# A hybrid transformer block on one core: weight sums loaded a unit ahead, the merge begun with the second half of the tokens, the last part of top-k in more steps

## The chip, the core and the metric

The kernel runs on one core of a Trainium2 chip. The core has five engines that run their own instruction streams: TensorE (PE in the profile; its weight loads are PEld), VectorE (DVE), ScalarE (ACT), GpSimd (POOL), and SyncE (SP), which here only issues DMAs. The order of the instructions on each engine is fixed when the program is built; at run time an instruction waits for what it needs and holds back all that stand behind it on its engine. The metric is the device time of one execution in microseconds (us), lower being better.

## The reference

One layer on a sequence of 1024 tokens and a width of 1024, all in float32:

```python
x = x + 1/2 * SwiGLU_1(RMSNorm(x))            # FFN1, hidden width 2816
h = RMSNorm(x); P = h @ W_in                  # one projection for all that follows
A = DSA sparse attention                      # indexer scores -> top 256 keys -> 8 heads
M = mLSTM matrix memory                       # conv, chunks of 64, stabilised scan
x = x + W_out( sigmoid(g_a) * (A @ W_a) + sigmoid(g_b) * (M @ W_b) )
x = x + 1/2 * SwiGLU_2(RMSNorm(x))            # FFN2
...
top_s, top_i = lax.top_k(score, k_sel)        # 256 keys of each query, from the indexer's scores
```

`g_a` and `g_b` are two slices of `P`. The fifth line is called the merge below.

## The kernel before

**Matmuls.** Each float32 product is made of three matmuls of rounded parts (high by high, high by low, low by high: `mm3`, L769, L770, L771). Before that an operand is split into a high and a low part: ScalarE rounds it (L898, L452, L185, L297), VectorE or POOL subtracts (L899, L453, L186, L298). The large products are done with sums of quarter blocks (products 0 to 6 in place of 8), so that the weights have to be added up as well as the activations.

**FFN1 and the weight sums.** `gate_up` (about 60 to 440 us) multiplies by the gate and up weights, `Down` (440 to 600 us) by the down weights. Beside them, `Presums` makes the sums of two later weights: 19 units of columns of `w_in` during `gate_up` (`step`, called once per column pair) and 4 units of rows of `w_out` during `Down` (`step_rows`). A unit takes two buffers of 1024 columns from the segments `plain` and `more` (11 pages in all, which everything else in these stages uses too), two loads of 512 KB on SP's queue (L371 for columns), four VectorE sums of 128x512 (L376, L377, L379, L380 for columns, L352, L353, L355, L357 for rows) and four stores of 256 KB to `d_s` or `d_o` on the same queue. The generator yields between these parts, so that the load of a unit is placed a call ahead of its sums.

In `Down`, L634 adds a psum into a tile of `h`, L606 and L613 add and subtract such tiles on VectorE, and L648 does so on POOL, on 128x1024.

**Mixing.** The projections run beside the top-k search on VectorE and ScalarE. The generator `topk` yields a share of a step, by which the loop that runs it decides how much to place beside each piece of the projections. Its last part takes, for each block j of 128 queries, a mask of the 256 best keys: a count (L1540 to L1542), a scan (L1544), two combining operations (L1546, L1547), and two ScalarE copies. L1205, L1237 and L1242 are VectorE's evictions of the projections' psum there.

**Attention and merge.** The attention ends, at about 1362 us, in steps of two product matmuls (L2124, L2125), an eviction of 64x512 on ScalarE (L2079), a normalising VectorE operation (L2084) and the split into `swap` (L898, L899) for the next product. `proj_b` multiplies M by W_b beside it; its last operations are L1928 on VectorE, and it holds the segment `h0` through `ybT` until it ends. `merge` then goes over eight weight blocks n, each in two halves of 512 tokens (`th`):

```python
sa, tb = ar.alloc(1024), ar.alloc(1024)      # L2176, L2177: 512 KB each, both halves
with self.tc.issue_after(self.split_A):      # not ahead of the last split of the attention
    nc.scalar.activation(y[th][c].f, sa.f[:, cs], AF.Sigmoid)      # L2181; y lies in h0
self.proj(w, yaT, th, ps)                    # 12 matmuls of 128x512
v.tensor_tensor(a, a, ps, ALU.mult)          # L2187; L2188 adds tb
```

The weights of W_a come through L846 and L185, the prepared weight sums of `w_out` through L431 and L452. After the merge FFN2 runs like FFN1, without weight sums.

**What sets the order.** The calls are written in the order above, but a scheduler with a simulated timeline decides, when the program is built, how each engine's instructions interleave; `issue_after` forbids it to place an instruction ahead of a named one.

Of the kernel before, what the change touches and what calls it, by code (L numbers as in the profile page):

```python
# [22 lines left out]
AF = mybir.ActivationFunctionType  # L23
# [295 lines left out]
class Presums:  # L319
# [6 lines left out]
    def __init__(self, k, w_in, d_s, w_out, d_o):  # L326
        self.k, self.w_in, self.d_s, self.w_out, self.d_o = k, w_in, d_s, w_out, d_o
        self.order = list(dict.fromkeys(i[0] for i in MIXING if i != "ik"))
        self.work, self.more = self.steps(), self.rows()

    def two(self):
        two = [None, None]
        while not all(two):
            two = [self.k.ar.alloc(1024, soft=True) for _ in range(2)]
            if not all(two):
                for b in two:
                    if b:
                        b.free()
                yield
        return two  # L340

    def rows(self):
        k, nc = self.k, self.k.nc
        for j in range(4):
            two = yield from self.two()
            for h in range(2):
                with k.tc.issue_after(k.mark):
                    nc.sync.dma_start(two[h].f, self.w_out[h * 512 + j * P:h * 512 + j * P + P, :])
            yield
            b11, b12, b21, b22 = (b.f[:, c:c + 512] for b in two for c in (0, 512))  # L350
            op = nc.vector.tensor_tensor
            op(b11, b12, b11, ALU.subtract)  # L352
            op(b12, b22, b12, ALU.subtract)  # L353
            yield
            op(b22, b22, b11, ALU.subtract)  # L355

            op(b21, b21, b22, ALU.subtract)  # L357
            for q, b in ((4, b11), (6, b12), (5, b22), (3, b21)):
                nc.sync.dma_start(self.d_o[j, Outs.SLOT[q]], b)
            for b in two:  # L360
                b.free()

    def steps(self):
        k, nc = self.k, self.k.nc
        for p in self.order:
            two = yield from self.two()
            v = [b.f.rearrange("p (k y c) -> p k y c", k=4, y=2) for b in two]
            for h in range(2):
                src = self.w_in[h * 512:h * 512 + 512, PAIRS[p]:PAIRS[p] + 256].rearrange("(k p) c -> p k c", p=P)
                with k.tc.issue_after(k.mark):  # L370
                    nc.sync.dma_start(two[h].f.rearrange("p (k c) -> p k c", k=4), src)  # L371
            yield
            a11, a21 = (v[0][:, :, y] for y in range(2))
            a12, a22 = (v[1][:, :, y] for y in range(2))
            op = nc.vector.tensor_tensor
            op(a22, a21, a22, ALU.add)  # L376
            op(a21, a11, a21, ALU.subtract)  # L377
            yield
            op(a11, a22, a11, ALU.subtract)  # L379
            op(a12, a12, a11, ALU.subtract)  # L380
            for q, b in ((5, a11), (6, a21), (2, a12), (4, a22)):
                nc.sync.dma_start(self.d_s[p, self.SLOT[q]].rearrange("p (k c) -> p k c", k=4), b)
            for b in two:
                b.free()
# [298 lines left out]
class Block:  # L683
# [814 lines left out]
    def topk(self, js, share):  # L1498
# [29 lines left out]
        for j in range(n):  # L1528
# [22 lines left out]
            yield 0.4  # L1551
# [849 lines left out]
```

## Time and profile before

| | |
|---|---|
| three runs | 2120.27, 2124.79 and 2126.83 us, median 2124.79 us |
| profiled execution | own time 2123.45 us, span 2121.7 us from the first to the last instruction |
| busy | TensorE 96%, VectorE 78%, ScalarE 50%, POOL 18% of the span |
| mean granted TensorE clock | 0.990 |

The shares of busy time are means over stages with different limits. In a stage where TensorE is busy throughout, nothing else sets the time. Where its row has gaps, the view of its waits says which instruction of another engine it waited for, and that engine's own row says what that one had waited for. The granted clock of a stretch is the TensorE clock as a share of full speed.

### The profile page before, as it was taken

To read this page: it belongs to the slowest core of one execution; us is meant where nothing else is said; L and a number is where in the kernel's file an instruction comes from. 1 tells how busy PE (TensorE), PEld (TensorE's weight loads), DVE (VectorE), ACT (ScalarE), POOL (GpSimd) and SP (SyncE) were. 2 spreads that over 40 slices of the span, in tenths; PEclk is the share of its full clock that TensorE was granted. 3 is DMA by queue.
4 is the path that set the end of the run, shared out by engine and by line. 5 is a ranking of instruction groups with operands and counts; after the bars stand their busy time and mean duration, and the time that the engine had idled before them with its cause. 6 is when DMAs were issued, how large, how long until landed. Compare 5 with 4: busy or idle time off the path is not lost. (4 is left out here: it accounts for less than half of the span.)

```text
span 2121.7 us, 27881 instructions
## 1 busy us (share of the span) xinstructions
PE 2046.8 (96%) x9349; PEld 1675.9 (79%) x9349; DVE 1650.1 (78%) x2852; ACT 1055.6 (50%) x1968; POOL 383.5 (18%) x397
## 2 busy tenths in 40 slices
PE   7999999999999989999999999899999999999999
PEld 5788787888787768777777788688888888888887
DVE  7977887678866785998889788787987666669963
ACT  8332222334436564985786578745723333334442
POOL 1000000000304323343445545422000000000300
PEclk9999999999999999999999999999999999999999
DMA  5479885394644223366686312552333232377241
GB/s 184 145 248 300 274 273 163 130 359 137 213 136 140 75 76 102 107 182 176 179 270 201 110 50 76 208 194 77 122 134 110 94 110 100 109 276 265 90 144 40
DMA packets 281804, 338.30 MB, mean 159 GB/s; under 512 B 20941, under 2 KB 186429, under 8 KB 281661
## 3 DMA queue, kind: packets, MB, share of 16 engines
q1 hardware_dynamic: 281660, 336.53, 48.6%
q8 instruction: 73, 1.20, 0.2%
q14 instruction: 71, 0.57, 0.1%
HBM read 231.57 MB, written 104.89 MB: 159 GB/s over the span
## 5 line engine op out<-in xcount | busy, mean ns | idle before, releaser
L769 PE MATMUL psum<-h,round 128*128 128x512 f32 x656 | 261.5, 399 | 3.1 <-DVE plain L1061 2.2
L770 PE MATMUL psum<-h,round 128*128 128x512 f32 x656 | 259.8, 396 | 1.0 <-DVE h L899 0.8
L771 PE MATMUL psum<-h,round 128*128 128x512 f32 x656 | 258.6, 395 | 0.3 <-DVE round L298 0.3
L648 POOL TENSOR_TENSOR swap<-swap,h 128x1024 f32<-128x1024 f32 x12 | 32.8, 2771 | 1020.5 <-DVE h L634 1020.5
L512 POOL TENSOR_TENSOR round<-raw,round 128x512 fp32r<-128x512 f32 x108 | 147.7, 1374 | 155.9 <-ACT round L511 111.2
L769 PEld LDWEIGHTS psum<-h,round 128*128 128x128 f32 x656 | 124.3, 190 | 30.6 <-DVE plain L1061 2.8
L771 PEld LDWEIGHTS psum<-h,round 128*128 128x128 f32 x656 | 124.2, 189 | 27.8 <-issue 1.6
L770 PEld LDWEIGHTS psum<-h,round 128*128 128x128 f32 x656 | 124.4, 190 | 27.0 <-DVE h L899 1.5
L769 PE MATMUL psum<-swap,round 128*128 128x512 f32 x312 | 125.8, 404 | 11.2 <-DVE plain L1237 6.9
L770 PE MATMUL psum<-swap,round 128*128 128x512 f32 x312 | 124.1, 398 | 1.1 <-DVE swap L899 0.9
L771 PE MATMUL psum<-swap,round 128*128 128x512 f32 x312 | 123.8, 397 | 0.2 <-POOL round L512 0.2
L1563 DVE TENSOR_SCALAR_CACHE_REDUCE plain<-plain 128x384 bf16<-128x384 f32 (+1 forms) x124 | 100.3, 808 | 2.5
L898 ACT ACTIVATE round<-plain 128x512 fp32r<-128x512 f32 x74 | 46.2, 631 | 106.0 <-PE psum L770 98.7
L297 ACT ACTIVATE round<-plain 128x512 fp32r<-128x512 f32 x75 | 47.3, 632 | 94.4 <-PE psum L770 70.0
L511 ACT ACTIVATE round<-raw 128x512 fp32r<-128x512 f32 x108 | 66.6, 622 | 38.1 <-PE psum L770 26.0
L899 DVE TENSOR_TENSOR round<-plain,round 128x512 fp32r<-128x512 f32 x74 | 57.0, 776 | 32.6 <-ACT round L898 32.3
L769 PE MATMUL psum<-h,spare 128*128 128x512 f32 x200 | 78.8, 396 | 3.1 <-DVE plain L1061 2.6
L769 PEld LDWEIGHTS psum<-swap,round 128*128 128x128 f32 x312 | 59.8, 192 | 26.9 <-DVE plain L1237 7.8
L770 PE MATMUL psum<-h,spare 128*128 128x512 f32 x200 | 78.7, 393 | 1.9 <-DVE h L899 1.9
L769 PE MATMUL psum<-h,extra 128*128 128x512 f32 x200 | 78.3, 392 | 2.2 <-DVE plain L1205 1.6
L769 PE MATMUL psum<-side 128*128 128x512 f32 x204 | 79.4, 389 | 0.0
L770 PE MATMUL psum<-side 128*128 128x512 f32 x204 | 79.4, 389 | 0.0
(750 smaller groups left out, 6027.7 us busy)
## 6 DMA issues: line engine op xcount, KB each, us to landing
plain<-d_a SPq DMA_DIRECT2D x154, 256.0 KB
d_a<-plain SPq DMA_DIRECT2D x117, 256.0 KB
raw<-in_ffn_w_gate_dram SPq DMA_DIRECT2D x44, 512.0 KB
plain<-in_w_in_dram SPq DMA_DIRECT2D x37, 512.0 KB
d_s<-plain SPq DMA_DIRECT2D x74, 256.0 KB
raw<-d_s SPq DMA_DIRECT2D x74, 256.0 KB
h<-in_ffn_w_down_dram SPq DMA_DIRECT2D x66, 256.0 KB
raw<-in_w_in_dram SPq DMA_DIRECT2D x53, 256.0 KB
```

What stands on the lines that cost most here:

```text
L297: k.nc.scalar.activation(hi.r.rearrange("p (k c) -> p k c", k=4), src, AF.Copy)
L511: self.done_A = k.nc.scalar.activation(hi.r, raw.f, AF.Copy).ins
L512: k.nc.gpsimd.tensor_tensor(lo.r, raw.f, hi.f, ALU.subtract)
L648: k.nc.gpsimd.tensor_tensor(x(th, dh), x(th, dh), u, ALU.add)
L769: mm(ps, lhs[0], rhs[0], start=start, stop=False, skip_group_check=more)
L770: mm(ps, lhs[0], rhs[1], start=False, stop=False, skip_group_check=more)
L771: mm(ps, lhs[1], rhs[0], start=False, stop=stop, skip_group_check=more)
L898: self.split_A = self.nc.scalar.activation(hi, src, AF.Copy).ins
L899: self.nc.vector.tensor_tensor(lo, src, hi.bitcast(F32), ALU.subtract)
L1563: v.tensor_scalar(s.junk[:, :s.width[j]], s.sc[j], s.cand[:, j:j + 1], None, ALU.is_ge, ALU.add, accum_out=s.cnt[:, j:j + 1])
```

## The change

Three edits are made together. All arithmetic, all volumes and all other stages stay.

1. `Presums` holds one unit of work back: the generator `run` issues the loads of a unit, and only then the sums of the unit before. Two units, four pages, can be held at a time. If there is no room for the next unit's buffers, the waiting unit's sums go first. (The sums of columns are now L368, L369, L371 and L372, their loads L362; the sums of rows L392, L393, L395 and L397.)
2. `merge` takes the halves in another order: the second half of the tokens for n = 0 to 4, then the first half for n = 0 to 4, then both halves of n = 5 to 7. The pre-activations are loaded by half (256 KB instead of 512 KB), straight into their place in `h0`, and the sigmoid works in place. The sigmoids may now stand ahead of the last splits, but not ahead of the last exponential of the attention (`exp_A` instead of `split_A`). The weights of five blocks are held at a time.
3. The last part of `topk` is cut into five steps per block instead of three, with the same sum of shares (0.2 + 0.3 + 0.3 + 0.3 + 0.1 for 3 x 0.4). The two ScalarE copies become steps of their own, and two buffers are freed before the last of them.

```diff
+    def run(self, units):
+        waiting = []
+        for load, work in units:
+            while True:
+                two = [self.k.ar.alloc(1024, soft=True) for _ in range(2)]
+                if all(two):
+                    break
+                for b in two:
                     if b:
                         b.free()
+                if waiting:
+                    yield from waiting.pop(0)
                 yield
+            load(two)
+            yield
+            waiting.append(work(two))
+            if len(waiting) > 1:
+                yield from waiting.pop(0)
+        for w in waiting:
+            yield from w
...
             act.activation(sc[j], sc[j], AF.Copy, scale=one(s.sg, j))
+            yield 0.2
...
-            yield 0.4
+            yield 0.3
             v.tensor_tensor_scan(pre.f, eq.f, eq.f, 0.0, ALU.add, ALU.max)
-            yield 0.4
+            yield 0.3
             v.scalar_tensor_tensor(eq.f, pre.f, one(s.ngt, j), eq.f, ALU.is_le, ALU.mult)
             v.scalar_tensor_tensor(sc[j], sc[j], thr, eq.f, ALU.is_gt, ALU.add)
-            act.activation(sc[j], sc[j], AF.Copy, bias=NEG, scale=-NEG)
             eq.free()
             pre.free()
-            yield 0.4
+            yield 0.3
+            act.activation(sc[j], sc[j], AF.Copy, bias=NEG, scale=-NEG)
+            yield 0.1
...
-                nc.scalar.activation(p.f, p.f, AF.Exp, bias=nb, scale=sc, accum_out=su)
+                self.exp_A = nc.scalar.activation(p.f, p.f, AF.Exp, bias=nb, scale=sc, accum_out=su).ins
...
-        for n in range(8):
+        halves = [(n, 1) for n in range(5)] + [(n, 0) for n in range(5)]
+        halves += [(n, th) for n in range(5, 8) for th in range(2)]
+        for i, (n, th) in enumerate(halves):
             c = n // 2 + n % 2 * 4
-            w = self.w.get()
-            sa, tb = ar.alloc(1024), ar.alloc(1024)
-            nc.sync.dma_start(sa.f, self.d_sa[c])
-            nc.sync.dma_start(tb.f, self.d_tb[c])
...
+            if n not in ws:
+                ws[n] = self.w.get()
+            tb = ar.alloc(512)
+            a = y[th][c].f
+            cs = slice(th * 512, th * 512 + 512)
+            nc.sync.dma_start(a, self.d_sa[c, :, cs])
+            nc.sync.dma_start(tb.f, self.d_tb[c, :, cs])
+            with self.tc.issue_after(self.exp_A):
+                nc.scalar.activation(a, a, AF.Sigmoid)
+            ps = self.bank(4 + i % 4)
+            self.proj(ws[n], yaT, th, ps)
```

TensorE's order is the same before and after from the end of FFN1 to the end of the top-k search and again from the second half of the merge to the end of the program; it differs beside the weight sums, in the last part of top-k, and where attention and merge meet. Three places are shown.

**VectorE in `Down`, beside the sums of rows.** The names are the segments of the tiles; L899 (after: L918) makes the low parts of operands, L634 (after: L653) adds a psum into a tile of `h` that POOL's L648 then reads, and L606 and L613 (after: L625 and L632) combine such tiles. Before:

```order
L634 SCALAR_TENSOR_TENSOR h_3143<-psum,h_3143 128x1024 x2
L606 TENSOR_TENSOR plain<-h_3143,h_3062 128x512
L899 TENSOR_TENSOR extra<-plain,extra 128x512 x2
L352 TENSOR_TENSOR plain<-plain 128x512
L899 TENSOR_TENSOR round<-plain,round 128x512 x2
L613 TENSOR_TENSOR h_3143<-h_3143,h_3062 128x512
L899 TENSOR_TENSOR side<-plain,side 128x512
```

After:

```order
L653 SCALAR_TENSOR_TENSOR h_3143<-psum,h_3143 128x1024
L393 TENSOR_TENSOR plain<-plain 128x512
L625 TENSOR_TENSOR plain<-h_3143,h_3062 128x512
L653 SCALAR_TENSOR_TENSOR h_3143<-psum,h_3143 128x1024
L918 TENSOR_TENSOR extra<-plain,extra 128x512 x2
L395 TENSOR_TENSOR plain<-plain 128x512
L392 TENSOR_TENSOR plain<-plain 128x512
L632 TENSOR_TENSOR h_3143<-h_3143,h_3062 128x512
L918 TENSOR_TENSOR round<-plain,round 128x512 x2
L397 TENSOR_TENSOR plain<-plain 128x512
```

Between the first L634 of the pair and the low parts of `round` there stood one sum of rows (L352); now there are three (L393, L395, L392), and L613 (now L632) stands ahead of the low parts instead of behind them.

**TensorE where the attention ends.** L2124 and L2125 (after: L2145 and L2146) are the last products of the attention, L2070 its transposes; the matmuls on `swap` are the merge's. Before:

```order
L2124 MATMUL psum<-more,extra 128x512
L2125 MATMUL psum<-round,extra 128x512
L2070 MATMUL psum<-ident,plain 128x128 x4
L2125 MATMUL psum<-more,extra 128x512
L2124 MATMUL psum<-more,extra 128x512
L2125 MATMUL psum<-more,extra 128x512
L769 MATMUL psum<-swap,round 128x512
L769 MATMUL psum<-swap,spare 128x512
L770 MATMUL psum<-swap,round 128x512
```

After (the last of the merge's matmuls that moved, the attention's last two products, and what follows):

```order
L788 MATMUL psum<-swap,round 128x512
L789 MATMUL psum<-swap,round 128x512
L790 MATMUL psum<-swap,round 128x512
L2145 MATMUL psum<-more,extra 128x512
L2146 MATMUL psum<-more,extra 128x512
L788 MATMUL psum<-swap,round 128x512
L788 MATMUL psum<-swap,spare 128x512
```

Thirty-six matmuls of the merge, those of the second half of the tokens, moved ahead of the attention's last two products. The first row after those products now belongs to the first half of the tokens.

**ScalarE at the same place.** L2079 (after: L2100) is the eviction of the attention's products, L898 (after: L917) the split for the next one, L2181 (after: L2206) the merge's sigmoid, L452 (after: L471) and L185 the rounding of weights. Before:

```order
L2079 ACTIVATE h_8690<-psum 64x512
L898 ACTIVATE more<-psum 128x512
L2079 ACTIVATE h_8690<-psum 64x512
L898 ACTIVATE swap<-h_8690 128x128 x2
L185 ACTIVATE more<-raw 128x512
L2079 ACTIVATE h_8690<-psum 64x512
L452 ACTIVATE extra<-plain 128x512
L898 ACTIVATE swap<-h_8690 128x128 x4
L2181 ACT_TABLE_LOAD
L2181 ACTIVATE h_10186<-plain 128x512 x2
L452 ACTIVATE spare<-plain 128x512
L898 ACTIVATE round<-h_10186 128x512
```

After:

```order
L2100 ACTIVATE h_8690<-psum 64x512
L917 ACTIVATE more<-psum 128x512
L2100 ACTIVATE h_8690<-psum 64x512
L2206 ACTIVATE h_10186<-h_10186 128x512
L917 ACTIVATE swap<-h_8690 128x128 x2
L2206 ACTIVATE h_10186<-h_10186 128x512 x2
L185 ACTIVATE more<-raw 128x512
L2100 ACTIVATE h_8690<-psum 64x512
L471 ACTIVATE extra<-plain 128x512
L917 ACTIVATE swap<-h_8690 128x128 x2
L2206 ACTIVATE h_10186<-h_10186 128x512
L917 ACTIVATE swap<-plain 128x128 x2
```

The table load and all of the sigmoids stood behind the last L2079; now the table load stands ahead of the last five evictions, and 16 sigmoids stand between it and the last split on `swap`.

## Rows read from the trace of the kernel before

**Rows 1.** The page: the span, and each engine's busy time and instructions.

```profile
span 2121.7 us, 27881 instructions
...
PE 2046.8 (96%) x9349; PEld 1675.9 (79%) x9349; DVE 1650.1 (78%) x2852; ACT 1055.6 (50%) x1968; POOL 383.5 (18%) x397
```

**Rows 2.** Windows: from:to, length; busy PE, PEld, DVE, ACT, POOL; clock, DMA share, GB/s.

```profile
200.00:250.00 50.00, 46.71 (x198) 37.85 (x197) 41.19 (x69) 12.46 (x22) 0.00 (x0) 0.97 0.91 282
300.00:325.00 25.00, 22.81 (x101) 18.58 (x100) 19.43 (x33) 7.33 (x13) 0.00 (x0) 1.00 0.87 273
550.00:600.00 50.00, 46.19 (x202) 37.58 (x202) 43.91 (x55) 19.41 (x34) 13.63 (x6) 1.00 0.76 252
1100.00:1150.00 50.00, 43.02 (x178) 34.20 (x178) 45.84 (x57) 34.98 (x68) 22.18 (x15) 0.93 0.73 237
1150.00:1200.00 50.00, 44.85 (x200) 36.67 (x200) 44.24 (x58) 29.26 (x51) 30.87 (x18) 0.90 0.47 152
1340.00:1375.00 35.00, 27.97 (x131) 21.70 (x130) 24.10 (x69) 26.21 (x64) 18.15 (x27) 0.90 0.70 246
1375.00:1425.00 50.00, 50.00 (x222) 41.42 (x221) 45.10 (x65) 19.10 (x34) 6.41 (x5) 1.00 0.65 229
```

**Rows 3.** TensorE's waits: total us, times, longest.

```profile
PE psum L769 <- DVE plain L1237: 6.9, 2, 3.8
...
PE psum L769 <- DVE plain L1061: 4.8, 2, 2.6
...
PE psum L2124 <- DVE h L2084: 3.7, 2, 3.0
```

**Rows 4.** VectorE's waits, 80 to 560 us.

```profile
DVE plain L376 <- DMA plain<-in_w_in_dram: 18.5, 8, 6.0
```

**Rows 5.** Timelines of VectorE and TensorE at 242 us: start, us, operation, [idle before].

```profile
242.26 0.69 DVE L376 TENSOR_TENSOR plain<-plain 128x512 f32<-128x512 f32 x1 [5.96 <-DMA plain<-in_w_in_dram]
...
243.60 0.50 PE L769 MATMUL psum<-h,spare 128*128 128x512 f32 x1 [2.64 <-DVE plain L1061]
```

**Rows 6.** Timelines of POOL, VectorE and TensorE, 546 to 565 us.

```profile
546.82 16.39 POOL L648 TENSOR_TENSOR swap<-swap,h 128x1024 f32<-128x1024 f32 x6 [513.70 <-DVE h L634]
...
547.73 2.03 DVE L606 TENSOR_TENSOR plain<-h,h 128x512 f32<-128x512 f32 x1
...
549.69 5.70 DVE L899 TENSOR_TENSOR extra<-plain,extra 128x512 fp32r<-128x512 f32 x2
555.31 2.89 DVE L352 TENSOR_TENSOR plain<-plain 128x512 f32<-128x512 f32 x1
558.12 5.64 DVE L899 TENSOR_TENSOR round<-plain,round 128x512 fp32r<-128x512 f32 x2
563.68 0.68 DVE L613 TENSOR_TENSOR h<-h,h 128x512 f32<-128x512 f32 x1
...
563.82 0.50 PE L770 MATMUL psum<-round 128*128 128x512 f32 x1 [2.73 <-DVE round L899]
```

**Rows 7.** TensorE's timeline around the end of the attention.

```profile
1359.68 0.47 PE L2124 MATMUL psum<-more,extra 128*128 128x512 f32 x1 [2.97 <-DVE h L2084]
...
1362.24 0.80 PE L769 MATMUL psum<-swap,round 128*128 128x512 f32 x1 [1.42 <-ACT swap L898]
...
1373.87 0.39 PE L769 MATMUL psum<-swap,round 128*128 128x512 f32 x1
```

**Rows 8.** Timelines there of VectorE, ScalarE, DMA queue; a window as above.

```profile
1346.40 0.69 DVE L1928 TENSOR_TENSOR h<-h,psum 128x512 f32<-128x512 f32 x1
...
1363.93 1.28 ACT L2181 ACT_TABLE_LOAD   x1
1365.22 1.15 ACT L2181 ACTIVATE h<-plain 128x512 f32<-128x512 f32 x2
...
1337.43 5.79 SPq L2176 DMA_DIRECT2D plain<-d_sa  x2
...
1347.20:1363.90 16.70, 10.12 (x46) 6.67 (x44) 11.99 (x30) 13.77 (x34) 11.81 (x12) 0.92 0.69 220
```

More of the change, by code (lines that the diff above doesn't have):

```diff
@@ L328, in __init__ @@
         self.order = list(dict.fromkeys(i[0] for i in MIXING if i != "ik"))
[L329 to L335, printed above, removed]
+        self.work, self.more = self.run(self.columns()), self.run(self.rows())
+    def run(self, units):
[5 more added lines that the diff above has]
+                    break
                 for b in two:
@@ L338, in two, with columns, load, work @@
                         b.free()
+                if waiting:
+                    yield from waiting.pop(0)
                 yield
-        return two
+            load(two)
[5 more added lines that the diff above has]
+            yield from w
+    def columns(self):
+        k, nc = self.k, self.k.nc
+        op = nc.vector.tensor_tensor
+        for p in self.order:
+            def load(two, p=p):
+                for h in range(2):
+                    src = self.w_in[h * 512:h * 512 + 512, PAIRS[p]:PAIRS[p] + 256].rearrange("(k p) c -> p k c", p=P)
+                    with k.tc.issue_after(k.mark):
+                        nc.sync.dma_start(two[h].f.rearrange("p (k c) -> p k c", k=4), src)
+            def work(two, p=p):
+                v = [b.f.rearrange("p (k y c) -> p k y c", k=4, y=2) for b in two]
+                a11, a21 = (v[0][:, :, y] for y in range(2))
+                a12, a22 = (v[1][:, :, y] for y in range(2))
+                op(a22, a21, a22, ALU.add)
+                op(a21, a11, a21, ALU.subtract)
+                yield
+                op(a11, a22, a11, ALU.subtract)
+                op(a12, a12, a11, ALU.subtract)
+                for q, b in ((5, a11), (6, a21), (2, a12), (4, a22)):
+                    nc.sync.dma_start(self.d_s[p, self.SLOT[q]].rearrange("p (k c) -> p k c", k=4), b)
+                for b in two:
+                    b.free()
+            yield load, work
@@ L342, in rows @@
     def rows(self):
         k, nc = self.k, self.k.nc
+        op = nc.vector.tensor_tensor
         for j in range(4):
[L345 to L384, printed above, removed]
@@ new lines, in load, with work @@
+            def load(two, j=j):
+                for h in range(2):
+                    with k.tc.issue_after(k.mark):
+                        nc.sync.dma_start(two[h].f, self.w_out[h * 512 + j * P:h * 512 + j * P + P, :])
+            def work(two, j=j):
+                b11, b12, b21, b22 = (b.f[:, c:c + 512] for b in two for c in (0, 512))
+                op(b11, b12, b11, ALU.subtract)
+                op(b12, b22, b12, ALU.subtract)
+                yield
+                op(b22, b22, b11, ALU.subtract)
+                op(b21, b21, b22, ALU.subtract)
+                for q, b in ((4, b11), (6, b12), (5, b22), (3, b21)):
+                    nc.sync.dma_start(self.d_o[j, Outs.SLOT[q]], b)
+                for b in two:
+                    b.free()
@@ L386, in step @@
+            yield load, work
     def step(self):
@@ L2170, in merge @@
         outs = Outs(self, self.a["w_out"][0], self.d_o, y)
[L2171 to L2172 removed]
+        have, ws = set(), {}
+        halves = [(n, 1) for n in range(5)] + [(n, 0) for n in range(5)]
+        halves += [(n, th) for n in range(5, 8) for th in range(2)]
+        for i, (n, th) in enumerate(halves):
             c = n // 2 + n % 2 * 4
[L2174 to L2194 removed]
+            if n not in ws:
[9 more added lines that the diff above has]
+            self.proj(ws[n], yaT, th, ps)
+            v.tensor_tensor(a, a, ps, ALU.mult)
+            v.tensor_tensor(a, a, tb.f, ALU.add)
+            tb.free()
+            have.add((th, c))
+            if {(0, c), (1, c)} <= have:
+                for b in ws.pop(n):
+                    b.free()
+                outs.prime(0, have)
+                if c > 3:
+                    outs.sums(c - 4)
         for pair in self.aqT.values():
```

18 lines of the change are left out of this document (removed).

## Prediction

> **What bounds the kernel now.** I read the page first: the span is 2121.7 us and TensorE is busy for 96% of it [rows 1], so at most some 75 us can be had from its idle time, wherever that lies. The windows then show where it lies [rows 2]. In the stretch right behind the merge TensorE is busy for the whole 50 us; there nothing but TensorE sets the time, and an edit that moves other work in such a stretch is worth nothing. The change touches four places where that is not so. By window: 200 to 250 us, 3.3 us idle and a granted clock of 0.97; 300 to 325 us, 2.2 us idle; 550 to 600 us, 3.8 us idle; 1100 to 1200 us, 7.0 + 5.2 = 12.2 us idle and clocks of 0.93 and 0.90; 1340 to 1375 us, 7.0 us idle and 0.90. A clock below 1.00 is a mean: TensorE fell to the lower of its two levels (1.2 GHz) for a few us after a gap, and work issued then takes twice as long. What that costs I take as the missing share of the window: 0.03 x 50 = 1.5 us at 200 us, 3.5 + 5.0 = 8.5 us at 1100 us, 0.10 x 35 = 3.5 us at 1340 us. The view of TensorE's waits names the releasers [rows 3]: VectorE's evictions L1061 (in FFN1) and L1237 (in top-k), and L2084 at the attention's end; in the Down stage it is L899 [rows 6].
>
> The profiled execution took 2123.45 us, 1.75 us more than its span and 1.34 us under the median of the runs shown, 2124.79. The sum below is made against 2123.45. A measurement of this kernel can tell about 0.3% (6.4 us) from no change.
>
> **Columns of w_in a unit ahead.** VectorE waits 18.5 us in eight places at L376 for a load [rows 4]. TensorE feels only what queues behind: at 242.26 the sum had waited 5.96 us, the eviction L1061 came next on VectorE, and TensorE resumed at 243.60 after 2.64 us [rows 5]. So the gain is bounded not by 18.5 but by TensorE's loss in the two windows where this happens: 3.3 + 1.5 + 2.2 = 7.0 us [rows 2]. The other six waits are covered by TensorE's queue of matmuls already released. Holding a load for a unit does not remove the wait: the load still stands on SP's queue behind the stores of earlier sums, whose buffers it needs, and the DMA engines are at 0.91 of their time there [rows 2]. In the new order of VectorE there are on average 10.9 operations between the release of a load and its first sum, against 8.4 before; at the 0.69 us of such a sum [rows 5] that is 1.7 us of lead on waits of up to 5.96. A third of a wait gone, I take a bit under half of the 7.0: **-3 us**, between -7.0 and +3 (one more wait like that of 2.64, since two units hold four of the eleven pages that other work needs).
>
> **Rows of w_out a unit ahead.** From 546.82 POOL works 16.39 us on six additions [rows 6]. In that time VectorE's sums of 128x512 from SBUF take 2.8 to 2.9 us each (5.70 and 5.64 for two, 2.89 for L352), and 0.68 as soon as POOL is done (L613). TensorE waits for the low parts of `round`, made in 558.12 to 563.76, until 563.82, after 2.73 us. The new order puts L393, L392 and L395 in place of one L352 ahead of these, and L632 too. Two prices: if every operation more costs the 2.8 us of its neighbours, the three are 8.4 us, and a dip of the clock like that at 200 us, 1.5, may follow; if POOL's six additions end when they did, at 563.2, six of VectorE's two-input operations have passed by then as before, and what is left (L632 and two low parts) takes 0.68 each, which ends about 2 us later than before. The rows show six such operations beside six additions, so I take **+2 us**, with +10 as the far end. One sum of rows later in Down also waits for its load, but of the window's 3.8 us idle only 3.8 - 2.7 = 1.1 are left for that; with the lead as above I take half, **-0.5**.
>
> **Top-k in more steps.** Same work, same shares. From 1100 to 1200 us VectorE is busy 45.8 + 44.2 = 90.1 of 100 us, more than TensorE [rows 2]: it is the bound, and TensorE's waits for L1237 are waits for VectorE to reach it. The order moves one L1237 up by one VectorE operation and another by two, puts nine of TensorE's matmuls ahead of one of its gaps and ten and twelve behind two others; what stands ahead of the evictions as a whole is the same. VectorE's idle time, 9.9 us, is the most that a better interleaving could give; I take a fifth, **-2 us**. A loss is bounded by one wait like the longest, 3.8 [rows 3], and half a clock dip behind it: +5.
>
> **The merge.** In the present trace TensorE waits three times at the attention's end: 2.97 us before 1359.68 (for L2084), 1.42 before 1362.24 (for the split into `swap`), and shortly after, and then runs at half clock; in the window it loses 7.0 + 3.5 = 10.5 us [rows 2, 7]. The change puts 36 matmuls of the merge ahead of the attention's last two products. They take 36 x 50/222 = 8.1 us [rows 2] and would fill these waits, if what they need is there. It is not there early. The loads go straight into `h0`, which is free when `proj_b` is done, 1346.4 [rows 8]; 16 loads, and 8 more transfers among them on the queue, are 24 x 256 KB = 6.3 MB. At the 220 GB/s that this stretch moved with the DMA engines at 0.69 of their time [rows 8], full use gives an estimate of 319 GB/s, so the last lands 20 us later, about 1366. ScalarE then has table load and 16 sigmoids between its last evictions. It was busy 13.77 us from 1347.20 to 1363.90 [rows 8]; three operations of a sigmoid's size (0.575 us, the pair of 1.15) fall away from that stretch, and 1.28 + 16 x 0.575 = 10.5 come in: 13.77 - 1.7 + 10.5 = 22.5 us, so that the split for the first half of the tokens is done at about 1369.8. TensorE is then at the place that it reached at 1373.87 before (1362.24 and 36 matmuls on) [rows 7]. That is **-4 us**. Bounds: -10.5, all of the loss; above, nothing limits it but the loads (the last rival).
>
> The Trainium skill speaks against the early table load: "ScalarE: Activation LUTs", section "What ACT_TABLE_LOAD costs", puts a switch at 1283 ns plus a drain of about 1380 ns. The trace shows the first figure alone: the load took 1.28 us from 1363.93 and the first sigmoid began at 1365.22 [rows 8]. By the page, estimated, this part would be -2.6 and the sum 1.4 us higher; I go by the rows.
>
> **Sum.** -3 + 2 - 0.5 - 2 - 4 = -7.5 us: 2123.45 - 7.5 = **2116 us**, 0.35% less.
>
> **The rivals.** *Gains are given back (2121).* VectorE bounds top-k and the Down window eats the gain of the columns: 0 for top-k, -3 + 2 for the weight sums, and -1.5 for the merge if ScalarE's chain is 2.5 us longer than I add up. For it: nearly all of TensorE's waits here are for an engine that has as much to do as before. Against it: the wait at 1359.68 has idle TensorE time that matmuls fill.
>
> *The large gain (2106).* Columns -6, rows 0, top-k -4, merge -8: -18. It needs the clock dips to go with their gaps; for it, every low clock in the windows follows a gap. Against it, the lead of 1.7 us and the end of the loads into `h0`.
>
> *The loads are not ahead (2119).* The queue holds a unit's load behind the stores, so that it lands as late as now: columns 0, the Down window +2, the rest as in the forecast, -4.5.
>
> *Slower (2131).* The transfers into `h0` are the bound instead of ScalarE. In the present kernel two of the merge's 512 KB loads were issued at 1337.43 [rows 8], ahead of that time; now all wait for `proj_b`, in the same queue as the weights of FFN2. The sigmoids stand on ScalarE ahead of the attention's last five evictions, so a late load holds the attention too. If the last of the sixteen lands at 1380 instead of 1366, what follows it (1369.8 - 1366) ends at 1384, 10 us behind the present 1373.87 instead of 4 ahead: 2123.45 - 3.5 + 10 = 2130. It ends slower by more than the measurement's 0.3% from a landing at 1380 on, that is 6.3 MB at under 190 GB/s. For it: the stretch moved 220. Against it: the DMA engines were not full.
>
> **How the numbers follow.** Forecast 0.42, with a range of its own of 2112 to 2119 (faster 0.33, same 0.09); gains given back 0.26 (same); large gain 0.13 (faster); loads not ahead 0.07 (same); slower 0.12. Together faster 0.46, same 0.42, slower 0.12. The range from 2105 to 2127 leaves out the slower case and a third of the large gain.
>
> **What would show it.** Right: VectorE's waits at the columns' first sum well under 18.5 us but not gone; the gap before 243.60 shorter; TensorE's wait for the low parts of `round` in Down about 2 us longer than 2.73; less idle and a clock above 0.90 at the merge; the table load ahead of the last five evictions, with sigmoids waiting for loads only at first. Wrong: TensorE's wait in Down growing by 5 us or more; ScalarE idle for a DMA ahead of an eviction of the attention; a new gap in FFN1 by buffers that come late; a table load with a drain behind it.

## The result, and the profile after

The changed kernel took 2112.31 us (median of 6 runs, 2108.77 to 2114.01), the kernel before 2127.38 us beside it (6 runs, 2120.27 to 2130.12): a ratio of 0.993 with a 95% interval of 0.9913 to 0.9948, so faster by 0.7%. The forecast was 2116 us and faster. The profiled execution has a span of 2110.9 us against 2121.7 [rows 1]. That is 10.8 us less, where the medians differ by 15.1: the profiled execution of the kernel before, 2123.45 us, lies 3.9 us under the median of its six runs, and that of the changed kernel, 2112.66 us, 0.4 above its own. The traces below place the 10.8 us.

The page of the changed kernel, its span and busy times:

```profile
span 2110.9 us, 27903 instructions
...
PE 2044.5 (97%) x9349; PEld 1675.8 (79%) x9349; DVE 1652.0 (78%) x2852; ACT 1054.4 (50%) x1968; POOL 381.7 (18%) x397
```

The work is the same. TensorE idles 8.5 us less (66.4 against 74.9 of the span) and is busy for 2.3 us less, at a mean granted clock of 0.992 against 0.990. Its windows over the stretches of [rows 2], shifted to where the program now is (same columns):

```profile
200.00:250.00 50.00, 49.98 (x221) 41.07 (x220) 43.01 (x71) 14.31 (x25) 0.00 (x0) 1.00 0.99 313
300.00:325.00 25.00, 25.00 (x111) 20.47 (x111) 19.41 (x33) 7.22 (x13) 0.00 (x0) 1.00 0.85 263
545.00:595.00 50.00, 46.75 (x199) 38.25 (x198) 44.02 (x61) 19.16 (x34) 10.29 (x5) 0.97 0.82 273
1095.00:1145.00 50.00, 43.36 (x188) 34.39 (x187) 46.51 (x62) 36.89 (x72) 24.65 (x16) 0.97 0.75 244
1145.00:1195.00 50.00, 47.31 (x220) 38.90 (x219) 41.45 (x61) 28.28 (x50) 36.23 (x22) 0.90 0.55 167
1330.00:1365.00 35.00, 28.61 (x127) 21.77 (x126) 24.89 (x56) 26.68 (x62) 13.97 (x16) 0.92 0.83 281
```

The columns of `w_in` are done: TensorE is busy for all of the first two windows. Top-k improved (9.3 us idle in the two windows against 12.1, and a better clock in the first). Down and the merge hardly changed: 3.3 us idle against 3.8, at a clock of 0.97 against 1.00, and 6.4 against 7.0, at 0.92 against 0.90.

A ledger says it more closely. Every trace here holds 9349 matmuls, so the start of the n-th can be compared wherever the order on TensorE is the same at that point. The table gives start of the n-th matmul minus that of the kernel before, in us, for one profiled execution of each kernel (the experiments are described below; minus is earlier). One execution can lie off its median: that of e4 took 2122.40 us, 6.6 above the median of its six runs.

| n, and its start before | changed | e1 sums | e2 top-k | e3 merge | e4 sums, top-k | e5 top-k, merge | e6 sums, merge | e7 as e4, residual later |
|---|---|---|---|---|---|---|---|---|
| 1350, 326.8 (columns done) | -7.1 | -7.3 | +2.5 | +0.2 | -6.4 | +1.7 | -6.2 | -6.9 |
| 2400, 567.8 (behind POOL's additions) | -5.0 | -4.2 | +2.5 | +0.7 | -4.5 | +2.2 | -4.2 | -4.8 |
| 2550, 603.2 (Down done) | -6.4 | -5.6 | +3.2 | +1.5 | -5.9 | +2.0 | -5.5 | -6.1 |
| 4650, 1071.6 (ahead of top-k's last part) | -3.9 | -5.0 | +3.1 | -0.1 | -4.7 | +4.4 | -4.7 | -8.0 |
| 5250, 1220.0 (behind it) | -9.9 | -4.4 | -1.7 | +1.0 | -7.6 | -3.9 | -4.0 | -14.4 |
| 6150, 1397.7 (behind the merge) | -11.1 | -4.3 | +4.7 | +1.3 | -1.3 | -3.3 | -3.6 | -15.2 |
| 9150, 2071.4 (FFN2 nearly done) | -10.8 | -4.1 | +4.6 | +1.5 | -1.1 | -3.2 | -3.3 | -15.2 |

From 603 to 1072 us all of these run the same order on TensorE, and still drift by -1.9 to +2.5 us. That is not yet all that chance does: e9, described below, has the order of the kernel before on every engine from 330 us on, and drifts by +4.4 us there and by -1.7 from 1072 to 1220 us. So a step of some 4 us in one stretch of one execution shows nothing by itself.

The steps that repeat are larger, or repeat often. Every kernel with the first edit gains 6 to 7 us in the columns and gives 2 to 3 back beside POOL. From 1072 to 1220 us every kernel of the table with the top-k edit gains 3 to 8 us (differences of the two lines: -6.0, -4.8, -2.9, -8.3, -6.4), and none without it (+0.6, +1.1, +0.7). e11, with the same order there, gains 7.7. e4 and e7 have one order on every engine until 1345 us, and gain 2.9 and 6.4: the spread is chance, the mean of the six is 6.0 us. In e8, e10 and e12, where sums of rows are moved and the scheduler's order differs from there on, TensorE's too, the stretch gains only 1.4 to 2.5 us, which chance alone can do. So the gain is shown for the order that came out, not for the edit in any order. And the kernels with the top-k edit and the old merge, e2 and e4, lose 6.4 us again before 1398 us.

### The profile page after: what moved, and what is told of

Its sections match the earlier page's. It is cut to its first block, busy times and chain, and to the rows that moved or that the text cites. A ratio compares the mean times of both kernels' runs of the same rounds, so it can differ in the third digit from the quotient of the medians.

```text
span 2110.9 us, 27903 instructions
## 1 busy us (share of the span) xinstructions
PE 2044.5 (97%) x9349; PEld 1675.8 (79%) x9349; DVE 1652.0 (78%) x2852; ACT 1054.4 (50%) x1968; POOL 381.7 (18%) x397
## 4 chain that ended last, share of the span: by engine, by line
PE 77%; DVE 11%; DMA 5%; ACT 3%; issue 3%; POOL 1%; SPq 0%; DVEq 0%; ACTq 0%; POOLq 0%
PE psum L789 23%; PE psum L788 23%; PE psum L790 23%; DVE plain L1584 2%; PE psum L1472 1%; PE psum L1471 1%; PE psum L2091 1%; DVE h L918 1%; PE psum L2146 1%; PE psum L2145 1%; DMA plain<-d_tb 1%; PE psum L900 1%; DMA raw<-in_ffn_w_up_dram 0%; ACT plain L1501 0%; ACT plain L1610 0%
## 5 line engine op out<-in xcount | busy, mean ns | idle before, releaser
L788 PE MATMUL psum<-swap,round 128*128 128x512 f32 x328 | 130.9, 400 | 5.8 <-ACT swap L917 2.1
L789 PE MATMUL psum<-swap,round 128*128 128x512 f32 x328 | 129.6, 395 | 2.1 <-DVE swap L918 1.9
L790 PE MATMUL psum<-swap,round 128*128 128x512 f32 x328 | 129.1, 394 | 0.0
L917 ACT ACTIVATE round<-plain 128x512 fp32r<-128x512 f32 x74 | 46.2, 631 | 97.7 <-PE psum L789 90.8
L530 ACT ACTIVATE round<-raw 128x512 fp32r<-128x512 f32 x108 | 66.6, 623 | 29.0 <-PE psum L789 15.4
L790 PE MATMUL psum<-side 128*128 128x512 f32 x208 | 80.9, 389 | 0.0
L789 PE MATMUL psum<-side 128*128 128x512 f32 x208 | 80.9, 389 | 0.0
L788 PE MATMUL psum<-side 128*128 128x512 f32 x208 | 80.9, 389 | 0.0
```

The costliest lines, as they stand in the source:

```text
L530: self.done_A = k.nc.scalar.activation(hi.r, raw.f, AF.Copy).ins
L788: mm(ps, lhs[0], rhs[0], start=start, stop=False, skip_group_check=more)
L789: mm(ps, lhs[0], rhs[1], start=False, stop=False, skip_group_check=more)
L790: mm(ps, lhs[1], rhs[0], start=False, stop=stop, skip_group_check=more)
L917: self.split_A = self.nc.scalar.activation(hi, src, AF.Copy).ins
```

## The experiments

Ratios are to the kernel before on the same chip, with their 95% interval.

**Each edit by itself.** e1 has the first edit alone, e2 the third, e3 the second, e4 the first and the third.

> The kernel before with the first edit alone (weight sums of columns and of rows a unit ahead). Read from the two traces, the columns gave 7.6 us (the gaps at 202, 241 and 322 us and the slow stretch behind the second), the six additions of POOL in Down took 2 back and the gap at 591 us gave 1.4: 7 us faster in all, ratio 0.9967. By the forecast's own terms it is 1.5 us faster, ratio 0.9993. If the order of the instructions in FFN1 is what counts, TensorE's time from 100 to 330 us is without a gap here too; if it was chance of one execution, gaps come back.

> The kernel before with the third edit alone (the last part of top-k in five steps). The traces of before and after differ by 7.3 us between the start and the end of this part: by that 7 us faster, ratio 0.9966. By the forecast's term 2 us faster, ratio 0.999. If VectorE bounds the stretch and only passes the gain on, no difference.

> The kernel before with the second edit alone (merge begun with the second half of the tokens). By the traces of before and after it moved the end of the merge by 0.5 us: same, ratio 0.9997, with ScalarE waiting some 3 us for the first load into h0 and TensorE still waiting at the attention's end. By the forecast's term 4 us faster, ratio 0.998.

> The changed kernel without its second edit (merge as before). If the merge gave nothing, this is as fast as the changed kernel: about 14 us under the kernel before, ratio 0.9932. If the forecast's terms were right and the rest came by chance, it is 3.5 us under, ratio 0.998.

| | median us | ratio |
|---|---|---|
| e1 sums | 2118.49 | 0.997 (0.9958 to 0.9981) |
| e2 top-k | 2127.80 | 1.0011 (1.0001 to 1.0021) |
| e3 merge | 2124.96 | 1.0005 (0.9996 to 1.0014) |
| e4 sums and top-k | 2115.83 | 0.9959 (0.9944 to 0.9975) |

e1 and e3 came as read from the traces. e2 and e4 did not: top-k alone is no faster at all, and e4 is 6 us slower than the whole change by the ratios. In the ledger it loses 6.4 us between 1220 and 1398 us, at the old merge. In e4 the waits of VectorE from 1330 to 1380 us:

```profile
DVE h L2209 <- DMA plain<-d_tb: 10.0, 1, 10.0
```

In the kernel before the same wait (L2188 there) is 0.5 us, and three loads of `tb` stand ahead of the residual on the queue. And the timelines of the DMA queue and of TensorE in e4:

```profile
1354.21 4.75 SPq L2368 DMA_DIRECT2D h<-d_x  x8
1359.97 1.60 SPq L2198 DMA_DIRECT2D plain<-d_tb  x2
```

```profile
1372.71 0.79 PE L788 MATMUL psum<-round 128*128 128x512 f32 x1 [6.28 <-ACT round L917]
```

The new top-k order also shifted how the scheduler placed the attention and what follows: the merge's loads of `tb` now stand behind eight loads of 512 KB of the residual for FFN2, VectorE's addition waits for them, and TensorE stands for 6.3 us. e2, with the same order there, shows the same wait at 10.1 us and TensorE's at 6.4.

**Pairs with the new merge, and the old merge with the queue put right.** e5 is the changed kernel without the first edit, e6 without the third. e7 is e4 with the loads of the residual held behind the fourth block's load of `tb`; on every engine its order is that of e4 until 1345 us:

```diff
-        for t in range(8):
-            nc.sync.dma_start(xs[t].f, d_x[t])
...
+            tb_in = nc.sync.dma_start(tb.f, self.d_tb[c]).ins
...
+            if n == 3:
+                for t in range(8):
+                    with self.tc.issue_after(tb_in):
+                        nc.sync.dma_start(xs[t].f, d_x[t])
```

> The changed kernel without its first edit (weight sums as before). Theory: the top-k edit gains 5 to 6 us by the end of its stretch and lost them only at the old merge, whose additive halves (tb) came late there; the new merge loads those in halves ahead of the residual. Then this kernel is 5 us under the one before, ratio 0.9975, with no wait of VectorE for tb. Rival, the edits simply do not add: top-k alone was +3 and the merge alone 0, so +3, ratio 1.001.

> The changed kernel without its third edit (top-k as before). Theory: the weight sums' 6 us alone, since the new merge gave nothing to the old top-k: ratio 0.997. Rival, the merge needs the weight sums' edit to pay: 10 us or more under, ratio 0.995.

> The fourth experiment (weight sums and top-k edited, merge as before) with the eight 512 KB loads of the residual for FFN2 issued behind the loads of tb of the first four blocks of the merge instead of ahead of the second. Theory: VectorE's wait of 10.0 us for tb and TensorE's gap of 6.3 us behind it came from that order on the DMA queue alone; the gap is gone, the end of the merge comes 6 us earlier, ratio near that of the whole change (0.993). Rival: the queue holds tb for its buffers, or the DMA engines are full; then the wait stays, whatever the order, ratio 0.996.

e5 took 2120.60 us, ratio 0.9976 (0.9967 to 0.9985); e6 2118.95 us, 0.9968 (0.9956 to 0.9979); e7 2110.63 us, 0.9929 (0.9917 to 0.9941). All three came as the theory had it; e5 has no wait of VectorE for `tb`. In e7 VectorE's waits and the DMA queue read:

```profile
DVE h L2209 <- DMA plain<-d_tb: 2.7, 1, 2.7
```

```profile
1349.14 1.79 SPq L2198 DMA_DIRECT2D plain<-d_tb  x2
...
1359.34 4.70 SPq L2216 DMA_DIRECT2D h<-d_x  x8
```

So it was the place in the queue that held `tb`: the wait falls from 10.0 to 2.7 us, not to nothing, and TensorE's gap of 6.3 us is gone. The merge's new order is worth nothing by itself (e3, and e6 against e1), 6 to 7 us by the ratios beside the top-k edit (e2 to e5, e4 to the changed kernel), and those can be had by the old merge as well.

**Down: the sums beside POOL.** The changed kernel around POOL's six additions, from the timelines of POOL, VectorE and TensorE (they answer to [rows 6]):

```profile
538.45 16.42 POOL L667 TENSOR_TENSOR swap<-swap,h 128x1024 f32<-128x1024 f32 x6 [504.98 <-ACT extra L917]
```

```profile
537.09 1.22 DVE L653 SCALAR_TENSOR_TENSOR h<-psum,h 128x1024 f32<-128x1024 f32 x1
...
544.11 1.21 DVE L653 SCALAR_TENSOR_TENSOR h<-psum,h 128x1024 f32<-128x1024 f32 x1
545.25 4.58 DVE L918 TENSOR_TENSOR extra<-plain,extra 128x512 fp32r<-128x512 f32 x2
549.75 2.88 DVE L395 TENSOR_TENSOR plain<-plain 128x512 f32<-128x512 f32 x1
552.56 2.86 DVE L392 TENSOR_TENSOR plain<-plain 128x512 f32<-128x512 f32 x1
555.34 0.68 DVE L632 TENSOR_TENSOR h<-h,h 128x512 f32<-128x512 f32 x1
555.94 1.28 DVE L918 TENSOR_TENSOR round<-plain,round 128x512 fp32r<-128x512 f32 x2
```

```profile
557.28 0.80 PE L789 MATMUL psum<-round 128*128 128x512 f32 x1 [3.25 <-DVE round L918]
```

L393 and L625 ahead of these, the two `extra`, L395 and L392 are six operations with both inputs in SBUF; POOL is done at 554.9, and L632 and `round` run at full speed. L653, which has one input in psum, takes as long beside POOL (1.21 us) as ahead of it (1.22). By the ledger the stretch costs 2.1 us more than before, as forecast (+2). e8 leaves out the calls that place sums there:

```diff
-            if beside and i > 33 and i % 2:
+            if beside and i > 33 and i % 2 and not 35 <= i <= 41:
                 beside()
```

> The changed kernel with no sums of rows placed while POOL does its six additions in Down (the calls of the steps 35 to 41 are left out, so that the sums follow later). Theory: each two-input operation of VectorE beside POOL takes 2.8 us, and three of them stand ahead of the low parts of round; without them TensorE's gap of 3.4 us there is gone. Rival: POOL's length sets the gap, whatever VectorE does; it stays at 3. The order of the later stages differs from the changed kernel's, so the whole time is not compared, only this stretch.

VectorE's timeline of e8 there:

```profile
538.82 4.86 DVE L918 TENSOR_TENSOR extra<-plain,extra 128x512 fp32r<-128x512 f32 x2
543.60 5.69 DVE L918 TENSOR_TENSOR round<-plain,round 128x512 fp32r<-128x512 f32 x2
549.22 6.89 DVE L918 TENSOR_TENSOR side<-plain,side 128x512 fp32r<-128x512 f32 x4
```

The operations still take 2.8 us beside POOL, but `round` is now third and fourth in line and done at 549.3, and TensorE has no gap there. By the ledger the stretch from 327 to 568 us gains 3.1 us on the kernel before, where the changed kernel loses 2.1; the sums placed later bring gaps of 0.7 and 1.8 us, and 2.1 us are given back by 603 us. As a whole e8 took 2103.59 us, ratio 0.9895 (0.988 to 0.991). Most of that is not from Down: from 1220 to 1398 us its profiled execution gains 5.6 us, in another order of attention and merge, and 6.1 from 603 to 1072 us. e10 and e12 below have the order of e8 on every engine from the start to 1220 us and lose 0.4 and 1.0 us in that stretch, so the 6.1 are chance of that execution.

**The columns: is it the transfer's time?** e9 is the kernel before, its column loads cut to half (the other half of each buffer keeps old data, so that the sums are of other numbers):

```diff
-                    nc.sync.dma_start(two[h].f.rearrange("p (k c) -> p k c", k=4), src)
+                    nc.sync.dma_start(two[h].f.rearrange("p (k c) -> p k c", k=4)[:, :2], src[:, :2])
```

> The kernel before with half of each load of columns left out (the other half of the buffers keeps old data, so that the sums of w_in are of other numbers). Theory: TensorE's gaps at 202, 241 and 322 us come from VectorE's waits for these loads; with half the bytes the waits fall from 18.5 us to under 6, and TensorE is busy for all of 100 to 330 us: 7 us faster, ratio 0.9965. Rival: the place of the evictions in VectorE's queue makes the gaps, whatever the loads; two of the three gaps stay, ratio 0.999.

It took 2123.98 us, ratio 0.9983 (0.9971 to 0.9995). The theory fell and the rival came near: VectorE's waits for the loads went from 18.5 to 12.2 us only (L355 is the first sum here), and TensorE stays idle for 5.4 us of the 230, against 5.5 before:

```profile
DVE plain L355 <- DMA plain<-in_w_in_dram: 12.2, 6, 4.6
```

```profile
100.00:330.00 230.00, 224.62 (x985) 183.92 (x984) 188.92 (x309) 66.31 (x116) 0.00 (x0) 1.00 0.75 232
```

The test is not of the bytes alone. The scheduler placed other instructions elsewhere before 330 us, on VectorE and the DMA queue above all. At the longest wait of each, in order of issue, the unit's second load was issued at 233.85 before and at 232.12 in e9, where VectorE's timeline reads:

```profile
237.15 0.69 DVE L355 TENSOR_TENSOR plain<-plain 128x512 f32<-128x512 f32 x1 [4.64 <-DMA plain<-in_w_in_dram]
```

From issue to sum it is 8.4 us before (to 242.26, [rows 5]) and 5.0 with half the bytes. But VectorE was free for the sum 2.4 us after the issue before, and 0.4 us after it in e9. So fewer bytes do land sooner, and being issued 2.0 us nearer to its use gave more than half of that away. The changed kernel moves all bytes and waits as long as before, in VectorE's waits from 80 to 560 us:

```profile
DVE more L368 <- DMA more<-in_w_in_dram: 6.3, 3, 4.5
...
DVE plain L368 <- DMA plain<-in_w_in_dram: 5.7, 5, 3.5
...
DVE plain L368 <- issue: 4.9, 3, 2.6
```

The rows that name the unit's load make 12.0 us, against 18.5 before; all idle time ahead of the first sums is 19.1 us, against 19.4 (with 4.9 now and 0.9 before put down to no releaser, and 2.2 now to a load of gate weights). And yet TensorE has no wait at all from 100 to 330 us. What differs is the order around the wait. Timelines of VectorE and of TensorE in the changed kernel, at the place of [rows 5]:

```profile
238.44 0.69 DVE L368 TENSOR_TENSOR more<-plain,more 128x512 f32<-128x512 f32 x1 [4.53 <-DMA more<-in_w_in_dram]
239.12 0.69 DVE L1080 TENSOR_TENSOR plain<-plain,psum 128x512 f32<-128x512 f32 x1
...
240.33 0.68 DVE L1080 TENSOR_TENSOR plain<-plain,psum 128x512 f32<-128x512 f32 x1
```

```profile
239.86 0.50 PE L788 MATMUL psum<-h,spare 128*128 128x512 f32 x1
```

and in the kernel before:

```profile
242.87 0.68 DVE L1061 TENSOR_TENSOR plain<-more,psum 128x512 f32<-128x512 f32 x1
```

```profile
238.08 0.39 PE L769 MATMUL psum<-h,spare 128*128 128x512 f32 x1
```

The eviction at 239.12 releases the matmul at 239.86, and TensorE has just come there: it has 21 matmuls on `extra` ahead of those on `spare` where it had 12. Nine at 0.23 us are 2.0 us; in its old order it would have stood there for about that long (an estimate from these rows). The eviction that it waited for before, at 242.87, is the next along VectorE, at 240.33 now. VectorE came to the sum 2.4 us earlier, waited 1.4 us less, and has one more eviction between. So at this place TensorE's own order hides the wait that is left. No run has one of the orders without the other; they come together in every kernel with the first edit.

**The merge: why its own gain is small.** In the changed kernel TensorE's timeline at the end of the attention (it answers to [rows 7]):

```profile
1357.94 0.50 PE L788 MATMUL psum<-swap,round 128*128 128x512 f32 x1 [2.09 <-ACT swap L917]
...
1361.33 0.80 PE L789 MATMUL psum<-swap,round 128*128 128x512 f32 x1 [1.90 <-DVE swap L918]
```

The wait of 2.97 us [rows 7] is filled by the merge's matmuls, and two new ones stand behind it. On ScalarE the first load into `h0` is late (first fence), and on VectorE the operations of two halves of the merge, n = 3 and 4, stand ahead of the attention's last three normalisations, L2105 (second):

```profile
1337.30 1.28 ACT L2206 ACT_TABLE_LOAD   x1 [2.85 <-DMA h<-d_sa]
1338.59 1.15 ACT L2206 ACTIVATE h<-h 128x512 f32<-128x512 f32 x2
```

```profile
1351.65 0.69 DVE L2209 TENSOR_TENSOR h<-h,psum 128x512 f32<-128x512 f32 x1 [0.97 <-PE psum L790]
1352.37 1.45 DVE L2210 TENSOR_TENSOR h<-h,plain 128x512 f32<-128x512 f32 x1
1353.74 0.84 DVE L2105 TENSOR_TENSOR h<-psum,h 64x256 f32<-64x256 f32 x2
...
1358.19 0.67 DVE L2209 TENSOR_TENSOR h<-h,psum 128x512 f32<-128x512 f32 x1
1358.89 0.69 DVE L2210 TENSOR_TENSOR h<-h,plain 128x512 f32<-128x512 f32 x1
1359.50 0.84 DVE L2105 TENSOR_TENSOR plain<-psum,h 64x256 f32<-64x256 f32 x2
```

e11 is the changed kernel with these four placed behind the last L2105 (`norm_A`); on every engine its order is that of the changed kernel until 1330 us. e12 has this and the edit of e8, and e10 the edits of e7 and e8:

```diff
-            v.tensor_tensor(a, a, ps, ALU.mult)
-            v.tensor_tensor(a, a, tb.f, ALU.add)
+            with self.tc.issue_after(self.norm_A) if i in (3, 4) else nullcontext():
+                v.tensor_tensor(a, a, ps, ALU.mult)
+                v.tensor_tensor(a, a, tb.f, ALU.add)
```

> Experiments 7 and 8 together: weight sums and top-k edited, no sums beside POOL's six additions, the merge as before but with the residual's loads behind those of tb. If the two gains add (8 was some 7 us under the changed kernel, 7 was 2 us under it), ratio 0.988 to 0.989; if what 8 gained lies in the order of later stages that this kernel changes again, 0.992.

> The changed kernel with the merge's VectorE operations of two halves (n = 3 and 4, second half of the tokens) placed behind the attention's last normalising operation instead of ahead of it. Theory: the attention's last split came late because these operations (1.3 us) and ScalarE's sigmoids stood ahead of it; TensorE's last two gaps there, 2.4 and 2.2 us, shrink by 1 to 2 us in all. As the whole time moves by less than the measurement tells, the verdict goes by the gaps: ratio 0.992 to 0.993. Rival: the chain from product to eviction to split alone sets them, and they stay.

> The changed kernel with both: no sums beside POOL's additions (experiment 8) and the merge's operations behind the attention (experiment 11). Theory: ratio 0.989 as in 8 or 1 us less. If 8 owed its time to chance in the order of the later stages, this one, whose order differs again at the merge alone, keeps it; a ratio of 0.992 or more would speak against 8.

e10 took 2112.20 us, ratio 0.992 (0.9906 to 0.9935); e11 2103.19 us, 0.9878 (0.9863 to 0.9893); e12 2104.92 us, 0.9883 (0.9867 to 0.99). The expectation of e11 was right in kind and far too small, e12 came as expected, and of the two outcomes named for e10 it was the second. VectorE there, and the window of the merge:

```profile
1354.53 0.85 DVE L2105 TENSOR_TENSOR plain<-psum,h 64x256 f32<-64x256 f32 x2 [1.23 <-ACT h L2100]
```

```profile
1325.00:1360.00 35.00, 32.36 (x159) 25.81 (x158) 24.75 (x66) 28.30 (x66) 14.82 (x21) 1.00 0.81 266
```

Both gaps are gone and the clock stays at 1.00; TensorE idles 2.6 us of 35 where the changed kernel idled 6.4 at a clock of 0.92. In the ledger e11 gains 7.9 us between 1220 and 1398 us (-12.7 to -20.7) and e12 8.0 (-9.9 to -17.8), the changed kernel 1.2. ScalarE's wait for the first load is still there (3.1 us against 2.8), so it was not what held TensorE. e10 is no better than e7: what e8 gained beyond Down lay in its order of the merge, which e10 does not have, and in the chance named above. e11 is the fastest kernel here together with e8 and e12; these three don't differ by more than their intervals.

## Why the prediction was right, point by point

**The time** was forecast at 2116 us within 2105 to 2127, and faster; 2112.31 us lies inside. That it came so near is in part luck: 7.5 us of change were forecast, and the medians differ by 15.1. The sum started from 2123.45 us, an execution 3.9 us under the median of six, and that hid part of the miss. In the ledger of the two traces the terms made up for one another only in part; beside them it has +0.6 ahead of the columns and +2.5 between Down and top-k, where no edit acts:

- **Columns, -3:** mis-sized. The ledger shows -7.7 and -7.6 from 80 to 327 us in the changed kernel and e1, all of the bound of 7.0 with the clock dip. The lead of "1.7 us on waits of up to 5.96" was not the fault: at 242 us the wait fell by 1.4 us. The step that failed is the next, "a third of a wait gone" taken as the share of TensorE's loss that goes. All idle time ahead of the first sums hardly shrank (19.4 to 19.1 us) and TensorE's went to nothing; at 242 us its own new order, nine more matmuls ahead of the one that needs the eviction, hides what is left of the wait. "Well under 18.5" holds for the rows that name the load (12.0), not for the idle time as a whole. That the load "still stands behind the stores" may be so, but at 233.85 it was issued 2.4 us before VectorE was free for the sum: there the wait was for the landing.
- **Rows beside POOL, +2:** right in size (2.1 in the ledger) and in mechanism (six operations beside six additions). The price per operation would have given 8.4. TensorE's wait itself grew only from 2.73 to 3.25; the rest is a dip of the clock behind it (0.97 in the window), which the forecast had only in its far price.
- **Sums later in Down, -0.5:** it was -1.4; the gap of 1.1 us ahead of 592.4 is gone.
- **Top-k, -2:** mis-sized. Six executions in this order gain 2.9 to 8.3 us in the stretch. "A fifth" of VectorE's idle time was a choice with no row behind it. In the trace TensorE's waits for the eviction L1237 (now L1256) went from 6.9 us to 2.9, and a new wait of 3.5 us for the rounding of weights (L530) stands there.
- **Merge, -4:** it did not come. The new order improves on the old by 1.2 us in its stretch, within chance, and alone by nothing (e3). ScalarE's chain, by which I timed it, was not the last: the first load came 2.85 us late without effect, and VectorE operations that the sum did not have, those of two halves, stood ahead of the last normalisations. With them placed behind, the stretch gains 7.9 us (e11). The early table load took 1.28 us, with the sigmoid right behind it. So the drain of the Trainium skill ("ScalarE: Activation LUTs", "What ACT_TABLE_LOAD costs") does not show behind the load here either.
- **What no term had:** the edits are not independent. The sum of their ratios alone is -0.3 + 0.11 + 0.05 = -0.14%, the whole is -0.7%. The first edit adds to the others (e5 to the changed kernel: 0.9976 to 0.993). With the top-k edit the scheduler puts `tb` behind the residual under the old merge, and the new merge avoids that. I priced the three edits one by one against the old order, which misses this.

**The rivals.** "Gains are given back" did not hold for the whole, but it is what happened to the top-k edit alone, by a mechanism that I had not named. "Slower" had the loads into `h0` as the bound: they were late for 2.85 us, once. "Not ahead" fell with the columns. "The large gain" (2106) was not reached by the change, but by e8, e11 and e12, after further edits.

**What stays open.** Why top-k's finer steps gain some 6 us is shown only as far as the stretch, the edit and the waits named above; which of its pieces does it was not tried. In the columns no run has TensorE's new order without VectorE's, and only one of the three gaps was followed. The traces place 10.8 of the 15.1 us between the medians; the rest lies in the choice of executions. The order changes of the scheduler beyond the edited place are shown by their effect (e2, e4, e7), not explained.

## What to carry to other kernels

When a scheduler or a queue fixes the order as a whole, test edits in pairs: an edit that gains in its own stretch can lose as much where its new order meets a later one, and a second edit may only undo that. Where work is filled into a stall, look on every engine for what stands ahead of the last step of the chain that stalls; there moving four operations of VectorE, 3.5 us in all, gained 6.7 us by the ledger (7.9 against 1.2). The length of a wait on a helper engine is not its cost (19.4 and 19.1 us here, with 5.5 and 0 us idle on TensorE); see when the operation that TensorE needs behind it begins. And before a step of a few us in one trace is called a gain, compare it with what two executions of the same order differ by.

## What the runs showed of the hardware

- VectorE's operations of 128x512 with two inputs from SBUF go one for one with POOL's additions of 128x1024: up to 2.9 us each instead of 0.68, six beside six, in all fourteen traces. An operation with one input in psum is not held (1.21 us beside POOL, 1.22 ahead of it). How many of the first kind stand ahead of the needed one counts, not the total; e8 gained by bringing the needed ones up to third and fourth place.
- At the merge TensorE's granted clock was 0.50 of full speed, the lower level of 1.2 GHz, from 1359.3 to 1366.1 us in the changed kernel, right behind a gap of 2.1 us and four matmuls; the second gap, of 1.9 us, lies within that stretch. In e11, without these gaps, the clock stayed at 1.00. A window of the changed kernel:

```profile
1360.00:1365.00 5.00, 3.67 (x9) 2.90 (x10) 2.44 (x7) 1.55 (x4) 1.61 (x1) 0.50 0.79 236
```

- Halving the bytes of late loads took 6.3 of 18.5 us off VectorE's waits and 0.1 off TensorE's idle time from 100 to 330 us, in an order that issued them nearer to their use.
- Two executions of kernels with the same order on every engine can drift apart by some 4 us in a stretch of 470 us: +4.4 us in e9 against the kernel before, from 603 to 1072 us.
